# Part of the dense tokens of a PEER layer gather their expert rows, four slots of a token on the partitions

## The chip, the cores and the metric

The kernel runs on 1 core of one Trainium2 chip. The metric is the device time of one execution in microseconds. Runs of the kernel before took 3018.54 us at the median of three (3012.81 to 3020.27). The profile shows one execution; durations, waits and clocks below come from it.

Names: TensorE is PE, its weight loads PEld, VectorE is DVE, ScalarE is ACT, GpSimd is POOL, SyncE is SP. DMAs issued by SP and by POOL share 16 DMA engines.

## The reference, cut to what matters

The reference is an encoder of two layers on 512 tokens of width 1024. A layer is an input projection, two groups of attention heads, an output projection, a layer norm, a PEER feed-forward and another layer norm. The change touches the PEER part:

```python
q = (xc @ wq).reshape(PEER_CHUNK, PEER_HEADS, 2, half)
sc = jnp.einsum('chpd,hpnd->chpn', q, sub_keys, ...)
s1, i1 = lax.top_k(sc[:, :, 0], PEER_TOPK)
s2, i2 = lax.top_k(sc[:, :, 1], PEER_TOPK)
...                                   # the best 16 of 16 x 16 sums: top_s, eidx
g = jax.nn.softmax(top_s, axis=-1)
u_sel = jnp.take(u, eidx, axis=0)
a = jax.nn.gelu(jnp.einsum('chkd,cd->chk', u_sel, xc, ...), approximate=False)
w = (g * a).astype(x.dtype)
v_sel = jnp.take(v, eidx, axis=0)
return jnp.einsum('chk,chkd->cd', w, v_sel)
```

There are 8 heads with 16 experts each, so 128 slots a token, out of 16384 experts. Each expert has one row of u and one of v, of 1024 floats.

## The kernel before, in words

The 512 tokens are four chunks of 128. Chunk 0 (`gat`) takes its PEER part by **gathering**; chunks 1 to 3 (`dense`, 384 tokens, `ND`) take it **dense**, over all 16384 experts in 128 blocks (`NB`) of 128.

Dense, for a block: TensorE multiplies the block's u rows with the tokens and ScalarE takes the gelu, which gives a tile `ge` of 128 experts by 384 tokens (`acts`, L841 to L859). The gates of the chosen experts stand in a table G in DRAM, block by block, zero where an expert was not chosen; `w_` = G times `ge` (L1085). `w_` is the stationary operand that combines the block's v rows into six PSUM banks `accb`, 128 tokens by 512 columns each, over all 128 blocks (`combine`, L1043 to L1050). To keep fp32 precision with the fast fp32r matmul, u, v, `w_` and the tokens are split in a high and a low part, and three products are summed: a block has 8 x 3 matmuls of 384 columns for the activations and 6 x 3 of 512 columns for the combination. ScalarE casts the high parts (uh L850, vh L1081, wh L1088) and VectorE subtracts for the low ones (ul L851, vl L1082, wl L1089).

G is written by `spread` (L893): 48 steps of 8 tokens, one-hot products by VectorE, 16 matmuls of 128 f16 columns, copies by ScalarE into a tile `stg`, and a DMA of each group of 32 tokens. During the spread the activations of the first 24 blocks (`LEAD`) run ahead, and a ring of 24 `ge` buffers holds them. In the main loop (L1057) the activations of block b+24 come beside the combination of block b, so blocks 0 to 103 have 42 matmuls and blocks 104 to 127 only 18. The last six are held back to the end.

Gathering, for chunk 0: 256 indirect DMAs in a layer (L1005), issued by POOL. Each brings one row of u or v per token, token t on partition t, 128 rows of 4 KB. For u a VectorE instruction multiplies and sums the row with the token (`ujob`, L1009), for v another adds the weighted row to one of two accumulators (`vjob`, L1017). Before them comes the ranking of chunk 0 (`rank`, L966, 37 steps on VectorE). Four buffers (`slots`, L956) are used in turn.

The order: ranking steps, 128 u jobs, 128 v jobs and 7 closing steps form one list of 300 `jobs` (L1032 to L1034). `pace` (L1055) says how many of them follow each block: weight 4 for blocks 1 to 103, 1 for 104 to 121. All jobs of a block stand behind its `wl`. VectorE's order in the main loop is the written one (`manual_schedule`, L1056); the other engines' queues are ordered by the framework's planner. The u and v blocks come by SP, two blocks to a DMA of 1 MB (L844, L884), with four buffers `wst` for both; G by one DMA for four blocks (L888).

Of the kernel before, what the change touches and what calls it, by code (L numbers as in the profile page):

```python
# [48 lines left out]
def encoder_kernel(ctx: ExitStack, tc: tile.TileContext, x, ln_in_g, ln_in_b, w_in, qn_g, kn_g, sink,  # L49
# [152 lines left out]
    for l in range(L):  # L202
# [638 lines left out]
        def acts():  # L841

            for g2 in range(NB // 2):
                ut = load_w(peer_ut[l, g2], "ut")  # L844
                for bi in range(2):
                    us = ut[:, bi * D:(bi + 1) * D]
                    b = mm_bank("ps_a")
                    uh = up.tile([P, KD, P], F32R, tag="uh", name="uh")
                    ul = up.tile([P, KD, P], F32R, tag="ul", name="ul")
                    act.copy(uh.rearrange(ff), us)  # L850
                    v.tensor_tensor(out=ul.rearrange(ff), in0=us, in1=uh.rearrange(ff).bitcast(F32), op=SUB)  # L851
                    for k in range(KD):
                        pe.matmul(b[:, :ND], uh[:, k, :], xTh[:, k, :], start=k == 0, stop=False)  # L853
# [39 lines left out]
        def spread():  # L893
            for c in dense:
                for tg in range(P // TG):
                    stg = (sp, lp)[tg % 2].tile([P, NB, TG], F32, tag="stg", name="stg", bufs=1)
                    for t8 in range(TG // 8):
# [12 lines left out]
                        v.tensor_tensor(out=o12, in0=bc(iota2[:, None, :, :], sh2), in1=bc(iu[:, :, None, :], sh2), op=EQ)  # L910
                        v.tensor_tensor(out=a_h, in0=o1, in1=tv(gh), op=MUL)
                        v.tensor_tensor(out=a_l[:, :3], in0=o1[:, :3], op=MUL,
                                        in1=bc(gl[:, o:o + 6].rearrange("p (q t) -> p q t", t=2)[:, :, None, :], [P, 3, P, 2]))
                        for t in range(2):
                            act.activation(a_l[:, 3, :, t], o1[:, 3, :, t], AF.Copy, scale=glf[:, o + 6 + t:o + 7 + t])
                        for q in range(2):
                            b = acc_bank("ps_g")
                            for t in range(4):
                                bs = b[:, t * P:(t + 1) * P]
                                r, e = q * 2 + t // 2, t % 2  # L920
                                pe.matmul(bs, o2[:, r, :, e], a_h[:, r, :, e], start=True, stop=False)  # L921
                                pe.matmul(bs, o2[:, r, :, e], a_l[:, r, :, e], start=False, stop=True)  # L922
# [36 lines left out]
        def slot():  # L959
            used[0] += 1  # L960
            return slots[:, used[0] % 4, :]
        for c in gat:
# [37 lines left out]
            acc = [ep.tile([P, D], F32, tag=f"gacc{i}", name="gacc", bufs=1) for i in range(2)]  # L1000
            ep.tile([P, 112], BF16, tag="line", name="line", bufs=1)

            def gather(src, j, idx=idx):
                t = slot()
                pool.indirect_dma_start(out=t, out_offset=None, in_=src,  # L1005
                                        in_offset=bass.IndirectOffsetOnAxis(ap=idx[:, j:j + 1], axis=0))
                return t

            def ujob(j, c=c, a_=a_, w_=w_, gather=gather):  # L1009
                t = gather(peer_u, j)  # L1010
                v.tensor_tensor_reduce(out=t, in0=t, in1=h[:, c, :], op0=MUL, op1=ADD, scale=1.0,  # L1011
                                       scalar=0.0, accum_out=a_[:, j:j + 1])
# [4 lines left out]
            def vjob(j, acc=acc, w_=w_, c=c, gather=gather):  # L1017
                t = gather(peer_v, j)
                if j < 2:
                    v.tensor_scalar(acc[j], t, w_[:, j:j + 1], None, op0=MUL)  # L1020
                else:
                    v.scalar_tensor_tensor(acc[j % 2], t, w_[:, j:j + 1], acc[j % 2], op0=MUL, op1=ADD)  # L1022
# [32 lines left out]
        pace = [0 if b < 1 or b >= NB - 6 else 4 if b < NB - LEAD else 1 for b in range(NB)]  # L1055
        with tc.manual_schedule(engines={mybir.EngineType.DVE}):  # L1056
            for g2 in range(NB // 2):  # L1057
                if g2 > 0:
# [7 lines left out]
                for bi in range(2):  # L1066
# [21 lines left out]
                    act.copy(wh, wf)  # L1088
                    v.tensor_tensor(out=wl, in0=wf, in1=wh.bitcast(F32), op=SUB)  # L1089
# [7 lines left out]
                    while done < want:  # L1097
                        f, j = jobs[done]
                        f(j)
                        done += 1  # L1100
# [82 lines left out]
```

## Time and profile before

| | value |
|---|---|
| median of three runs | 3018.54 us |
| the profiled execution | 3019.66 us, span 3017.9 us |
| PE busy, PEld busy | 98%, 90% |
| DVE, ACT, POOL busy | 81%, 43%, 27% |
| moved by DMA | 749.46 MB, 248 GB/s over the span |
| granted TensorE clock | 0.996 |

A row of instructions gives the line, the engine, the operation, the tile that is written and those that are read, and the shape; in a group, the count, the busy time, the mean time of one in ns, then the idle time of the engine just ahead of it and what ended that. Ends of matmuls are modelled, and consecutive ones overlap, so the time from one start to the next is what one costs. A window row gives the busy time of each engine in a stretch, the granted clock, the mean busy share of the 16 DMA engines and the GB/s.

### The profile page before, as it was taken

How to read it: one execution, taken by the hardware profiler on the slowest of the kernel's cores; microseconds unless marked ns; L12 is line 12 of the kernel's file. 1: busy time of each engine (PE TensorE's matmuls, PEld its weight loads, DVE VectorE, ACT ScalarE, POOL GpSimd, SP SyncE). 2: the span in 40 equal slices, each digit the busy share in tenths (PEclk: the TensorE clock that was granted, in tenths of full speed). 3: DMA queues.
4: the chain of work that ended last, by engine and by line, in shares of the span. 5: the costliest groups of instructions: out<-in, count | busy, mean ns of one | idle time of the engine just before them, and what ended most of it. 6: DMA issues, size and time to landing. Idle time of an engine off the chain costs nothing.

```text
span 3017.9 us, 47799 instructions
## 1 busy us (share of the span) xinstructions
PE 2952.6 (98%) x18034; PEld 2716.3 (90%) x18034; DVE 2435.1 (81%) x5084; ACT 1310.7 (43%) x2642; POOL 820.7 (27%) x524
## 2 busy tenths in 40 slices
PE   7999999999999999999999999999999999999998
PEld 7899899999999999998898998999999999998986
DVE  6777999778887888888777789997787887787887
ACT  4665168443333333333247641783433333333332
POOL 0000000015555555553000000000255555555630
PEclk9999999999999999999999999999999999999999
DMA  5014667659999989998420247775689989888982
GB/s 196 29 57 151 235 254 280 214 207 335 327 326 330 329 322 328 331 338 301 149 98 15 73 164 273 259 262 205 236 318 339 334 317 335 323 318 310 330 298 91
DMA packets 262232, 749.46 MB, mean 248 GB/s; under 512 B 19952, under 2 KB 130288, under 8 KB 231792
## 3 DMA queue, kind: packets, MB, share of 16 engines
q1 hardware_dynamic: 188272, 477.94, 44.4%
q0 software_dynamic: 73728, 268.47, 24.9%
q8 instruction: 141, 2.31, 0.3%
q14 instruction: 91, 0.75, 0.1%
HBM read 691.81 MB, written 54.53 MB: 247 GB/s over the span
## 4 chain that ended last, share of the span: by engine, by line
PE 85%; DVE 12%; ACT 1%; issue 1%; DMA 1%; SPq 0%; DVEq 0%; ACTq 0%
PE ps_a L855 12%; PE ps_a L854 12%; PE ps_a L853 12%; PE ff L1050 11%; PE ff L1048 11%; PE ff L1049 11%; PE ps_o L417 2%; PE ps_g L922 2%; PE ps_g L921 2%; DVE ix L573 1%; PE ps_pt L403 1%; PE ps_s L379 1%; DVE sv L571 1%; PE ps_m L447 1%; DVE wql L511 1%
## 5 line engine op out<-in xcount | busy, mean ns | idle before, releaser
L1005 POOL DMA_INDIRECT gt<-in_dram,idx x512 | 811.2, 1584 | 1913.5 <-ACT vh L1081 1206.4
L855 PE MATMUL ps_a<-xT,ul 128*128 128x384 f32 x2048 | 689.1, 336 | 1.8 <-DVE ul L851 1.8
L854 PE MATMUL ps_a<-xT,uh 128*128 128x384 f32 x2048 | 688.7, 336 | 0.0
L853 PE MATMUL ps_a<-xT,uh 128*128 128x384 f32 x2048 | 688.7, 336 | 0.0
L1048 PE MATMUL ff<-vh,wh 128*128 128x512 f32 x1440 | 561.3, 390 | 1.9 <-ACT wh L1088 1.9
L1050 PE MATMUL ff<-vh,wl 128*128 128x512 f32 x1440 | 562.6, 391 | 0.0
L1049 PE MATMUL ff<-vl,wh 128*128 128x512 f32 x1440 | 560.6, 389 | 0.0
L1081 ACT CAST vh<-vt 128x1024 fp32r<-128x1024 f32 x240 | 251.9, 1051 | 492.8 <-PE ff L1050 252.5
L854 PEld LDWEIGHTS ps_a<-xT,uh 128*128 128x128 f32 x2048 | 385.0, 188 | 9.6
L853 PEld LDWEIGHTS ps_a<-xT,uh 128*128 128x128 f32 x2048 | 385.2, 188 | 8.0
L855 PEld LDWEIGHTS ps_a<-xT,ul 128*128 128x128 f32 x2048 | 385.1, 188 | 2.1 <-DVE ul L851 2.1
L1082 DVE TENSOR_TENSOR vl<-vt,vh 128x1024 fp32r<-128x1024 f32 x240 | 293.5, 1223 | 108.7 <-ACT vh L1081 107.3
L1088 ACT CAST wh<-w 128x384 fp32r<-128x384 f32 x240 | 123.6, 515 | 575.8 <-DVE w L1085 575.8
L1022 DVE SCALAR_TENSOR_TENSOR gacc<-gt,gw,gacc 128x1024 f32<-128x1024 f32 x252 | 314.6, 1281 | 54.8 <-DMA gt<-in_dram,idx 54.3
L1011 DVE CUSTOM_DVE_ANT_0 gt<-gt,h 128x1024 f32<-128x1024 f32 x256 | 304.6, 1222 | 43.7 <-DMA gt<-in_dram,idx 43.4
L851 DVE TENSOR_TENSOR ul<-ut,uh 128x1024 fp32r<-128x1024 f32 x256 | 312.4, 1220 | 26.4 <-ACT uh L850 26.4
L1050 PEld LDWEIGHTS ff<-vh,wl 128*128 128x128 f32 x1440 | 270.5, 188 | 56.9
L850 ACT CAST uh<-ut 128x1024 fp32r<-128x1024 f32 x256 | 269.5, 1053 | 120.0 <-PE ps_a L854 112.4
L1048 PEld LDWEIGHTS ff<-vh,wh 128*128 128x128 f32 x1440 | 270.4, 188 | 50.9 <-ACT wh L1088 2.7
L1049 PEld LDWEIGHTS ff<-vl,wh 128*128 128x128 f32 x1440 | 270.5, 188 | 48.4
L1089 DVE TENSOR_TENSOR wl<-w,wh 128x384 fp32r<-128x384 f32 x240 | 134.0, 559 | 154.7 <-ACT wh L1088 154.7
L1085 DVE SCALAR_TENSOR_TENSOR w<-gg,ge 128x384 f32<-128x384 f32 x256 | 141.8, 554 | 0.0
(278 smaller groups left out, 4632.7 us busy)
## 6 DMA issues: line engine op xcount, KB each, us to landing
ut<-in_dram SPq DMA_DIRECT2D x128, 1024.0 KB
vt<-in_dram SPq DMA_DIRECT2D x128, 1024.0 KB
w_pq<-in_dram SPq DMA_DIRECT2D x48, 1024.0 KB
gg<-G SPq DMA_DIRECT2D x62, 768.0 KB
G<-stg SPq DMA_DIRECT2D x24, 1920.0 KB
w_o<-in_dram SPq DMA_DIRECT2D x24, 1024.0 KB
w_q<-in_dram SPq DMA_DIRECT2D x8, 1024.0 KB
gt<-in_dram,idx POOLq DMA_INDIRECT x512
```

The source lines that it names most:

```text
L850: act.copy(uh.rearrange(ff), us)
L851: v.tensor_tensor(out=ul.rearrange(ff), in0=us, in1=uh.rearrange(ff).bitcast(F32), op=SUB)
L853: pe.matmul(b[:, :ND], uh[:, k, :], xTh[:, k, :], start=k == 0, stop=False)
L854: pe.matmul(b[:, :ND], uh[:, k, :], xTl[:, k, :], start=False, stop=False)
L855: pe.matmul(b[:, :ND], ul[:, k, :], xTh[:, k, :], start=False, stop=k == KD - 1)
L1005: pool.indirect_dma_start(out=t, out_offset=None, in_=src, in_offset=bass.IndirectOffsetOnAxis(ap=idx[:, j:j + 1], axis=0))
L1011: v.tensor_tensor_reduce(out=t, in0=t, in1=h[:, c, :], op0=MUL, op1=ADD, scale=1.0, scalar=0.0, accum_out=a_[:, j:j + 1])
L1022: v.scalar_tensor_tensor(acc[j % 2], t, w_[:, j:j + 1], acc[j % 2], op0=MUL, op1=ADD)
L1048: pe.matmul(b, wh[:, cs], vh[:, ns], start=blk == 0, stop=False)
L1049: pe.matmul(b, wh[:, cs], vl[:, ns], start=False, stop=False)
L1050: pe.matmul(b, wl[:, cs], vh[:, ns], start=False, stop=blk == NB - 1)
L1082: v.tensor_tensor(out=vl, in0=vt[:, bi, :], in1=vh.bitcast(F32), op=SUB)
```

## The change

The last 32 tokens of chunk 3 (`NX` = 32) leave the dense activations and gather their rows, as chunk 0 does. Four slots of a token are brought at once: 32 tokens x 4 slots (`NQ` = 4) fill the 128 partitions, with slots 32q to 32q+31 of a token on partition group q. So 32 u gathers and 32 v gathers a layer serve them (`qujob`, `qvjob`). Before the loop the tokens, their indices and gates are copied to the four groups by 12 small DMAs. Each partition sums its own 32 slots in `qacc`; two fp32 matmuls (`qsum`) with a selection matrix `sel`, built once at the start, add the four groups and put the sum into the accumulator banks of chunk 3.

The activations have 352 columns (`NA`) in place of 384. The last 32 columns of `ge` are set to zero by POOL in each block, and the last group of G is set to zero in place of being spread: 44 steps in place of 48. `w_`, `wh`, `wl`, the reading of G and the combination keep all 384 tokens.

The list has 365 jobs: 32 qujobs; 37 ranking steps with 16 qvjobs between them; 16 qvjobs and two qsums; 128 u jobs, 128 v jobs, 6 closing steps. While chunk 0 is ranked, three buffers belong to the ranking, and the qvjobs use two (the last two of the ranking's 16 top steps end before a shared one is taken). After the ranking a fifth gather buffer is taken from the space of the former second accumulator; chunk 0's v jobs have one accumulator. Up to one job of a block is placed behind `ul` (`between`), another between `wh` and `wl`, and the rest behind the block's combination. The weights of `pace` are 3 for blocks 3 to 103 and 1 for 104 to 121.

```diff
+    NA = ND - NX
+    NQ = P // NX
...
+    sel = cp.tile([P, P], F32, name="sel")
+    v.tensor_scalar(sel, ident, 0.0, None, op0=MUL)
+    for q in range(NQ):
+        v.tensor_tensor(out=sel[:, P - NX:], in0=sel[:, P - NX:], in1=ident[:, q * NX:(q + 1) * NX], op=ADD)
...
+                    if between:
+                        between[0](len(gel) - LEAD)
                     for k in range(KD):
-                        pe.matmul(b[:, :ND], uh[:, k, :], xTh[:, k, :], start=k == 0, stop=False)
...
+                        pe.matmul(b[:, :NA], uh[:, k, :], xTh[:, k, :NA], start=k == 0, stop=False)
...
+                    pool.memset(ge[:, NA:], 0.0)
+                    act.activation(ge[:, :NA], b[:, :NA], AF.Gelu)
...
-        STEPS = ND // 8
+        STEPS = NA // 8
...
+                    if gi == NTG - 1:
+                        pool.memset(stg[:, :, TG - NX:], 0.0)
+                    for t8 in range((TG if gi < NTG - 1 else TG - NX) // 8):
...
+        to_rows(qc, *idx)
+        for q in range(NQ):
+            rs, js = slice(q * NX, (q + 1) * NX), slice(q * JQ, (q + 1) * JQ)
+            nc.sync.dma_start(qi[rs, :], idx[0][qr, js])
+            nc.sync.dma_start(hq[rs, :], h[qr, qc, :])
+            nc.sync.dma_start(qg[rs, :], gte[qr, qc, js])
+
+        def qujob(j):
+            t = gather(peer_u, qi[:, j:j + 1])
+            v.tensor_tensor_reduce(out=t, in0=t, in1=hq, op0=MUL, op1=ADD, scale=1.0,
+                                   scalar=0.0, accum_out=qa[:, j:j + 1])
+            if j == JQ - 1:
+                act.activation(qw, qa, AF.Gelu)
+                v.tensor_tensor(out=qw, in0=qw, in1=qg, op=MUL)
+
+        def qvjob(j, s):
+            t = gather(peer_v, qi[:, j:j + 1], s)
+            if j == 0:
+                v.tensor_scalar(qacc, t, qw[:, j:j + 1], None, op0=MUL)
+            else:
+                v.scalar_tensor_tensor(qacc, t, qw[:, j:j + 1], qacc, op0=MUL, op1=ADD)
+
+        def qsum(n):
+            ns = slice(n * 512, (n + 1) * 512)
+            pe.matmul(accb[qc, n], sel, qacc[:, ns], start=False, stop=False)
...
+                places_.append(lambda: ep.tile([P, D], F32, tag="gacc1", name="gt4", bufs=1))
...
-                if j < 2:
-                    v.tensor_scalar(acc[j], t, w_[:, j:j + 1], None, op0=MUL)
+                if j == 0:
+                    acc.append(ep.tile([P, D], F32, tag="gacc0", name="gacc", bufs=1))
+                    v.tensor_scalar(acc[0], t, w_[:, j:j + 1], None, op0=MUL)
                 else:
-                    v.scalar_tensor_tensor(acc[j % 2], t, w_[:, j:j + 1], acc[j % 2], op0=MUL, op1=ADD)
+                    v.scalar_tensor_tensor(acc[0], t, w_[:, j:j + 1], acc[0], op0=MUL, op1=ADD)
...
-            jobs += [(lambda j, ranks=ranks: next(ranks, None), j) for j in range(37)]
+            jobs += [(qujob, j) for j in range(JQ)]
+            rk = [(lambda j, ranks=ranks: next(ranks, None), j) for j in range(37)]
+            qv = [(lambda j: qvjob(j, 2 + j % 2 if j < 16 else None), j) for j in range(JQ)]
+            for i in range(37):
+                jobs += rk[i:i + 1] + (qv[i - 1:i] if 1 <= i < 17 else [])
+            jobs += qv[16:] + [(qsum, n) for n in range(2)]
...
+        def one(blk):
+            more(min(done[0] + 1, len(jobs) * sum(pace[:blk + 1]) // sum(pace)))
+
+        between.append(one)
+        pace = [0 if b < 3 or b >= NB - 6 else 3 if b < NB - LEAD else 1 for b in range(NB)]
...
                     act.copy(wh, wf)
+                    one(blk)
                     v.tensor_tensor(out=wl, in0=wf, in1=wh.bitcast(F32), op=SUB)
...
-                    want = len(jobs) * sum(pace[:blk + 1]) // sum(pace)
...
+                    more(len(jobs) * sum(pace[:blk + 1]) // sum(pace))
```

More of the change, by code (lines that the diff above doesn't have):

```diff
@@ L36 @@
 TG = 32
+NX = 32
 GB = 4
@@ L839, in encoder_kernel @@
         gel = []
+        between = []
         def acts():
@@ L851, in acts @@
                     v.tensor_tensor(out=ul.rearrange(ff), in0=us, in1=uh.rearrange(ff).bitcast(F32), op=SUB)
+                    if between:
+                        between[0](len(gel) - LEAD)
                     for k in range(KD):
-                        pe.matmul(b[:, :ND], uh[:, k, :], xTh[:, k, :], start=k == 0, stop=False)
-                        pe.matmul(b[:, :ND], uh[:, k, :], xTl[:, k, :], start=False, stop=False)
-                        pe.matmul(b[:, :ND], ul[:, k, :], xTh[:, k, :], start=False, stop=k == KD - 1)
+                        pe.matmul(b[:, :NA], uh[:, k, :], xTh[:, k, :NA], start=k == 0, stop=False)
+                        pe.matmul(b[:, :NA], uh[:, k, :], xTl[:, k, :NA], start=False, stop=False)
+                        pe.matmul(b[:, :NA], ul[:, k, :], xTh[:, k, :NA], start=False, stop=k == KD - 1)
                     ge = gp.tile([P, ND], F32, tag="ge", name="ge", bufs=LEAD)
-                    act.activation(ge, b[:, :ND], AF.Gelu)
+                    pool.memset(ge[:, NA:], 0.0)
+                    act.activation(ge[:, :NA], b[:, :NA], AF.Gelu)
                     gel.append(ge)
@@ L896, in spread @@
                     stg = (sp, lp)[tg % 2].tile([P, NB, TG], F32, tag="stg", name="stg", bufs=1)
-                    for t8 in range(TG // 8):
+                    gi = (c * P + tg * TG - T0) // TG
+                    if gi == NTG - 1:
+                        pool.memset(stg[:, :, TG - NX:], 0.0)
+                    for t8 in range((TG if gi < NTG - 1 else TG - NX) // 8):
                         gh, glf, gl, iT = flat[c]
@@ L957, in encoder_kernel, with slot, gather @@
         used = [0]
-        def slot():
+        places_ = [slots[:, i, :] for i in range(4)]
+        def slot(s=None):
+            if s is not None:
+                return slots[:, s, :]
             used[0] += 1
-            return slots[:, used[0] % 4, :]
-        for c in gat:
+            i = used[0] % len(places_)
+            if callable(places_[i]):
+                places_[i] = places_[i]()
+            return places_[i]
+        def gather(src, ix, s=None):
+            t = slot(s)
+            pool.indirect_dma_start(out=t, out_offset=None, in_=src,
+                                    in_offset=bass.IndirectOffsetOnAxis(ap=ix, axis=0))
+            return t
@@ L963, in encoder_kernel, with places, to_rows @@
+        def places(c):
             idx = ep.tile([P, J], I32, tag="idx", name="idx", bufs=1)
             fx = ep.tile([P, J], F32, tag="fx", name="fx", bufs=1)
+            return idx, fx
+        def to_rows(c, idx, fx):
+            v.tensor_scalar(fx, i1f[:, c, :], 128.0, float(l * NE), op0=MUL, op1=ADD)
+            v.tensor_tensor(out=idx, in0=fx, in1=i2f[:, c, :], op=ADD)
+        qc = dense[-1]
+        qr = slice(P - NX, P)
+        JQ = J // NQ
+        idx = places(qc)
+        ep.tile([P, J], F32, tag="ga", name="ga", bufs=1)
@@ new lines, in encoder_kernel @@
+        ep.tile([P, J], F32, tag="gw", name="gw", bufs=1)
+        qacc = ep.tile([P, D], F32, tag="gacc0", name="qacc", bufs=1)
+        hq = ep.tile([P, D], F32, tag="gacc1", name="hq", bufs=1)
+        ep.tile([P, 112], BF16, tag="line", name="line", bufs=1)
+        qi = ep.tile([P, JQ], I32, tag="qi", name="qi", bufs=1)
+        qg, qa, qw = (ep.tile([P, JQ], F32, tag=t, name=t, bufs=1) for t in ("qg", "qa", "qw"))
+        to_rows(qc, *idx)
[4 more added lines that the diff above has]
+            nc.sync.dma_start(qg[rs, :], gte[qr, qc, js])
@@ L966, in rank @@
+        def qsum(n):
+            ns = slice(n * 512, (n + 1) * 512)
+            pe.matmul(accb[qc, n], sel, qacc[:, ns], start=False, stop=False)
+        for c in gat:
+            idx, fx = places(c)
             def rank(c=c, idx=idx, fx=fx):
-                sx = slot()
+                sx = ep.tile([P, D], F32, tag="gacc1", name="sx", bufs=1)
                 n = 2 * PH * TK
@@ L978, in rank @@
                     yield from top_keys(st, hd, sc[hd // 4][:, hd % 4])
-                big = [slot() for _ in range(3)]
+                big = [slot(i) for i in range(3)]
                 tl = dict(ge=big[0].bitcast(F16), t1=big[1].bitcast(F16))
@@ L994, in rank @@
                 yield from soft(c, c + 1)
-                v.tensor_scalar(fx, i1f[:, c, :], 128.0, float(l * NE), op0=MUL, op1=ADD)
-                v.tensor_tensor(out=idx, in0=fx, in1=i2f[:, c, :], op=ADD)
+                to_rows(c, idx, fx)
+                places_.append(lambda: ep.tile([P, D], F32, tag="gacc1", name="gt4", bufs=1))
             ranks = rank()
@@ L999, in encoder_kernel, with ujob @@
             w_ = ep.tile([P, J], F32, tag="gw", name="gw", bufs=1)
[L1000 to L1010, printed above, removed]
+            acc = []
+            def ujob(j, c=c, a_=a_, w_=w_, idx=idx):
+                t = gather(peer_u, idx[:, j:j + 1])
                 v.tensor_tensor_reduce(out=t, in0=t, in1=h[:, c, :], op0=MUL, op1=ADD, scale=1.0,
@@ L1015, in ujob, with vjob @@
                     v.tensor_tensor(out=w_, in0=w_, in1=gte[:, c, :], op=MUL)
-            def vjob(j, acc=acc, w_=w_, c=c, gather=gather):
-                t = gather(peer_v, j)
-                if j < 2:
-                    v.tensor_scalar(acc[j], t, w_[:, j:j + 1], None, op0=MUL)
+            def vjob(j, acc=acc, w_=w_, c=c, idx=idx):
+                t = gather(peer_v, idx[:, j:j + 1])
+                if j == 0:
+                    acc.append(ep.tile([P, D], F32, tag="gacc0", name="gacc", bufs=1))
+                    v.tensor_scalar(acc[0], t, w_[:, j:j + 1], None, op0=MUL)
                 else:
-                    v.scalar_tensor_tensor(acc[j % 2], t, w_[:, j:j + 1], acc[j % 2], op0=MUL, op1=ADD)
+                    v.scalar_tensor_tensor(acc[0], t, w_[:, j:j + 1], acc[0], op0=MUL, op1=ADD)
             def tail(c=c, acc=acc):
-                v.tensor_tensor(out=acc[0], in0=acc[0], in1=acc[1], op=ADD)
-                yield
                 hc = h[:, c, :]
@@ L1031, in encoder_kernel @@
             steps = tail()
-            jobs += [(lambda j, ranks=ranks: next(ranks, None), j) for j in range(37)]
+            jobs += [(qujob, j) for j in range(JQ)]
[4 more added lines that the diff above has]
+            jobs += qv[16:] + [(qsum, n) for n in range(2)]
             jobs += [(ujob, j) for j in range(J)] + [(vjob, j) for j in range(J)]
-            jobs += [(lambda j, steps=steps: next(steps, None), j) for j in range(7)]
+            jobs += [(lambda j, steps=steps: next(steps, None), j) for j in range(6)]
         g_2 = bload(ln2_g[l], D, "ln_g")
@@ L1053, in encoder_kernel, with more @@
         parts = []
-        done = 0
-        pace = [0 if b < 1 or b >= NB - 6 else 4 if b < NB - LEAD else 1 for b in range(NB)]
+        done = [0]
+        def more(want):
+            while done[0] < want:
+                f, j = jobs[done[0]]
+                done[0] += 1
+                f(j)
+        def one(blk):
+            more(min(done[0] + 1, len(jobs) * sum(pace[:blk + 1]) // sum(pace)))
+        between.append(one)
+        pace = [0 if b < 3 or b >= NB - 6 else 3 if b < NB - LEAD else 1 for b in range(NB)]
         with tc.manual_schedule(engines={mybir.EngineType.DVE}):
@@ L1095, in encoder_kernel @@
                         parts.append((blk, wh, wl, vh, vl))
-                    want = len(jobs) * sum(pace[:blk + 1]) // sum(pace)
[L1097 to L1100, printed above, removed]
+                    more(len(jobs) * sum(pace[:blk + 1]) // sum(pace))
         for c in dense:
```

3 lines of the change are left out of this document (1 added, 2 removed).

## The prediction

> **What bounds the kernel now.** I read the busy shares first, then the chain that ended last, then the stages of layer 0 in a table of windows, and last the rows of single instructions. The page:
>
> ```profile
> PE 2952.6 (98%) x18034; PEld 2716.3 (90%) x18034; DVE 2435.1 (81%) x5084; ACT 1310.7 (43%) x2642; POOL 820.7 (27%) x524
> ...
> PEclk9999999999999999999999999999999999999999
> ...
> PE 85%; DVE 12%; ACT 1%; issue 1%; DMA 1%; SPq 0%; DVEq 0%; ACTq 0%
> ```
>
> TensorE is 98% busy at full granted clock and 85% of the chain. A busy PE is not yet a bound PE, so the stages (columns: stretch, length, busy time and count of PE, PEld, DVE, ACT, POOL, then clock, DMA share and GB/s):
>
> ```profile
> 403.00:555.00 152.00, 152.00 (x1355) 142.01 (x1354) 138.37 (x175) 119.01 (x247) 0.00 (x0) 1.00 0.72 268
> 555.00:660.00 105.00, 105.00 (x534) 95.75 (x533) 82.27 (x280) 41.94 (x55) 0.00 (x0) 1.00 0.49 170
> 660.00:1412.00 752.00, 752.00 (x3826) 686.89 (x3826) 606.12 (x748) 275.30 (x369) 394.11 (x255) 1.00 0.92 328
> 1412.00:1486.00 74.00, 74.00 (x327) 60.94 (x326) 59.50 (x86) 28.27 (x39) 4.34 (x3) 1.00 0.62 205
> ```
>
> They are the spread (the 48 steps that write G, with 24 expert blocks of matmul ahead), blocks 0 to 13 with the ranking of chunk 0, the 90 blocks with gathers, and the last blocks without activations. PE has no gap in any of them. But the third, half the time, runs DMA at 0.92 and DVE at 0.81 (606 of 752): neither is far behind. Starts of consecutive matmuls give their true price:
>
> ```profile
> 800.48 0.33 PE L853 MATMUL ps_a<-xT,uh 128*128 128x384 f32 x1
> ...
> 802.04 0.33 PE L853 MATMUL ps_a<-xT,uh 128*128 128x384 f32 x1
> ...
> 803.08 0.39 PE L1048 MATMUL ff<-vh,wh 128*128 128x512 f32 x1
> ...
> 804.90 0.39 PE L1050 MATMUL ff<-vh,wl 128*128 128x512 f32 x1
> ...
> 287.26 0.28 PE L551 MATMUL ps_pq<-xT,wql 128*128 128x256 f32 x1
> 287.38 0.28 PE L549 MATMUL ps_pq<-xT,wqh 128*128 128x256 f32 x1
> ...
> 449.38 0.22 PE L921 MATMUL ps_g<-ah,o 128*128 128x128 f16 x1
> ...
> 449.96 0.22 PE L922 MATMUL ps_g<-al,o 128*128 128x128 f16 x1
> ```
>
> The first pair lies nine starts apart, the second eight, the third one, the last ten: 384 columns go every 0.173 us, 512 every 0.227, 256 every 0.12, the 128 of f16 every 0.058. For the wide ones that is 13 ns and 0.417 ns a column. A block of 24 activation and 18 combining matmuls is 24 x 0.173 + 18 x 0.227 = 8.24 us. The weight load does not hold it: at 256 columns the pairs already go at 0.12.
>
> **The change, part by part.** *Narrower activations.* 352 columns: 0.160 us, so 0.32 us less per block, 7.92. Over 128 blocks and 2 layers that is 82 us, if PE stays the bound everywhere.
>
> *Spread.* 44 steps in place of 48. A step is 16 matmuls of 0.058 us, so four are 3.7 us of PE; 24 blocks ahead save 7.7. DVE, 138 of 152 us busy there, loses three instructions a step:
>
> ```profile
> L910 DVE TENSOR_TENSOR o<-iota,fl 128x2048 f16<-128x2048 f16 x48 | 56.6, 1220 | 0.6 <-PE ps_g L922 0.3
> L911 DVE TENSOR_TENSOR ah<-o,fl 128x1024 f16<-128x1024 f16 x48 | 32.9, 686 | 0.0
> ...
> L912 DVE TENSOR_TENSOR al<-o,fl 128x768 f16<-128x768 f16 x48 | 26.5, 553 | 0.0
> ```
>
> That is 2.46 us a step, 9.8 in all, so DVE does not hold the gain of 11.4 back by more than 1.6. I take 10 us a layer.
>
> *More gathers, sooner.* 64 more per layer, 320 in place of 256. Jobs go from 300 to 365. The old pace weights sum to 430, so a block at weight 4 takes 2.79 jobs; the new sum to 321, so one at weight 3 takes 3.41. Jobs 0 to 31 gather u for the 32 tokens (blocks 3 to 11), then come 37 ranking steps with 16 v gathers between them (12 to 27), then almost nothing but gathers to block 103 (76 blocks). Their bytes:
>
> ```profile
> q1 hardware_dynamic: 188272, 477.94, 44.4%
> q0 software_dynamic: 73728, 268.47, 24.9%
> ...
> ut<-in_dram SPq DMA_DIRECT2D x128, 1024.0 KB
> vt<-in_dram SPq DMA_DIRECT2D x128, 1024.0 KB
> ...
> gg<-G SPq DMA_DIRECT2D x62, 768.0 KB
> ...
> gt<-in_dram,idx POOLq DMA_INDIRECT x512
> ```
>
> A gather is 268.47 / 512 = 0.524 MB. ut and vt serve two blocks each and gg four: 1.245 MB a block. Before: 1.245 + 2.79 x 0.524 = 2.71 MB in 8.24 us, 329 GB/s, which is the 328 of the row. After: 1.245 + 3.41 x 0.524 = 3.03 MB; 7.92 us would need 383 GB/s. What can the queues do? Full busy is 477.94 MB in 44.4% of 3017.9 us, 357 GB/s, on average. Stretches that are already full, of 20 and of 8.25 us:
>
> ```profile
> 700.00:720.00 20.00, 20.00 (x106) 18.58 (x105) 14.70 (x21) 7.56 (x10) 11.08 (x7) 1.00 0.98 354
> 740.00:760.00 20.00, 20.00 (x104) 18.37 (x103) 15.99 (x22) 7.08 (x9) 9.77 (x8) 1.00 1.00 375
> 1100.00:1120.00 20.00, 20.00 (x102) 18.03 (x101) 16.02 (x17) 7.45 (x10) 9.13 (x7) 1.00 1.00 354
> ...
> 1000.00:1008.25 8.25, 8.25 (x44) 7.54 (x43) 6.96 (x11) 3.01 (x4) 5.37 (x4) 1.00 0.99 379
> 1008.25:1016.50 8.25, 8.25 (x44) 7.54 (x43) 5.45 (x10) 3.00 (x4) 3.21 (x4) 1.00 1.04 373
> 1066.00:1074.25 8.25, 8.25 (x44) 7.54 (x43) 5.79 (x7) 3.01 (x4) 2.68 (x2) 1.00 1.02 395
> ```
>
> The long ones mean 361, the short ones 382. I take the middle, 372: the backlog will be steady, but a stretch picked for being full flatters. So a gather block lasts 3.03 / 0.372 = 8.15 us, set by DMA and no longer by PE: 0.09 less than before, not 0.32. The ends are 8.51 (357 GB/s) and 7.92 (PE).
>
> *DVE.* One more job per 1.6 blocks, and jobs moved between ul and vl and between w and wl:
>
> ```profile
> L1011 DVE CUSTOM_DVE_ANT_0 gt<-gt,h 128x1024 f32<-128x1024 f32 x128 | 152.4, 1222 | 21.1 <-DMA gt<-in_dram,idx 20.9
> L1022 DVE SCALAR_TENSOR_TENSOR gacc<-gt,gw,gacc 128x1024 f32<-128x1024 f32 x121 | 151.0, 1282 | 17.2 <-DMA gt<-in_dram,idx 16.9
> ...
> L1082 DVE TENSOR_TENSOR vl<-vt,vh 128x1024 fp32r<-128x1024 f32 x92 | 112.6, 1224 | 46.9 <-ACT vh L1081 46.7
> ...
> L1089 DVE TENSOR_TENSOR wl<-w,wh 128x384 fp32r<-128x384 f32 x91 | 50.8, 559 | 58.3 <-ACT wh L1088 58.3
> ```
>
> These are groups of 660 to 1412. DVE is busy 606 / 752 x 8.24 = 6.64 us a block. It waits 0.64 for wh, 0.51 for vh and 0.42 for gathers. 0.62 more jobs of about 1.2 us make 7.39. A job in each gap covers the first two waits, which are worth nothing while PE is the bound and are needed now. Gather waits at today's rate are 0.52, in all 7.91: DVE just fits under 8.15. Behind a late gather stand, on DVE in its written order, vl, w and wl of the block, and behind these PE. The single accumulator in place of two makes adjacent v jobs dependent; 1.28 against a spacing of about 1.2 is under 0.1 us a block, within the 0.24 left.
>
> *Five buffers, and POOL.* The fifth keeps the time a buffer may take round at 5 / 3.41 blocks of 8.15, 12.0 us, where 4 / 2.79 x 8.24 was 11.8. That time is needed:
>
> ```profile
> 1002.77 1.68 POOL L1005 DMA_INDIRECT gt<-in_dram,idx  x1 [2.27 <-DVE ga L1011]
> ...
> 1010.89 1.25 DVE L1011 CUSTOM_DVE_ANT_0 gt<-gt,h 128x1024 f32<-128x1024 f32 x1 [0.28 <-DMA gt<-in_dram,idx]
> ...
> 1434.15 1.05 POOL L221 TENSOR_TENSOR tabs<-sin,gk 128x256 f32<-128x256 f32 x1
> ```
>
> Issue to use is 8 us with the queues full. POOL issues 3.41 x 1.55 (394.11 / 255) = 5.3 us a block, below 8.15. The new memset of 32 columns costs at most the 1.05 of the nearest POOL row; it waits for the buffer that w frees, and the next gather stands behind it on POOL. From nothing, where it runs when the buffer is already free, to an added gather wait on every block; I take nothing, the price stands with the third rival. The memset of a whole stg, 16 times that row's elements, is 1 to 17 us under the activation blocks that end the spread.
>
> *The small rest.* qsum: an fp32 matmul of 256 columns is two instructions of 0.216 us:
>
> ```profile
> 244.33 3.46 PE ps_m L447 x16
> ```
>
> So 512 columns are 0.87, two per layer 1.7 us; PE stands behind the last v job of the 32 tokens, once, covered by DVE's lead of about a block. SP issues 12 small DMAs before the loop, which wait for the indices; loads of vt and ut stand behind: 0 to 4 us at about 0.35 each, with the stg memset I take 1. The DVE work for the selection matrix is about 1 us once. In blocks 104 to 121 20 jobs remain in place of 12: 10 us more DVE on 59.5 of 74; I take 2.
>
> *Sum per layer:* spread -10; blocks 0 to 2, PE-bound, -1; blocks 3 to 11 at 8.15, -0.8; blocks 12 to 27 -2.5 (below); 76 gather blocks -6.8; rest +4.7. That is -16.4, two layers -32 with the 1 us. For blocks 12 to 27 the row is
>
> ```profile
> 640.00:660.00 20.00, 20.00 (x102) 18.18 (x102) 18.08 (x31) 8.01 (x11) 0.00 (x0) 1.00 0.44 156
> ```
>
> where the last ranking steps run: DVE 18.08 / 20 x 8.24 = 7.45 us a block, less 3.29 without jobs, over 2.79 steps is 1.5 us each. At 3.41 a block, with no v gathers between them, DVE needs 8.4 for about six blocks (+0.13 each); the other ten go at 7.92. The profiled execution took 3019.66 us, 1.1 above the median: 2987 or 2988 so, 2986 beside the median.
>
> **Rivals.** *1, PE keeps the pace.* The short full windows (382 on average, 395 once) say that 383 GB/s can be had; against it, these follow on idle stretches. Then 85 blocks gain 0.32: -27 in place of -7.6 a layer, 2948. The Trainium skill, "Perfetto Trace Analysis", section Roofline, says a lone core may draw more than its 358 GB/s share, to about 120%; by it DMA would not bind and this rival would hold; the trace agrees only in short windows.
>
> *2, slower: DMA stays at its average.* In the same 85 blocks at 357 GB/s, 8.51 us: +0.27 each, +23 a layer; with -8.8 for the rest +14, in all 3048. It decides from 368 GB/s down, where a block costs the old 8.24. For it: the average of both queues over the run (the gathers' 24.9% gives 357 too). The Trainium skill, "DMA: Bandwidth & Descriptors", Specifications, gives about 358 GB/s as a core's HBM limit; by that a block would be 8.47. The trace's 375 over 20 us stands above it.
>
> *3, gathers land later still.* If DVE waits 2.5 times today's 0.52 a block, it needs 8.69: +34 over 76 blocks, +24 a layer, 3067. It decides from 1.6 times. For it: 8 us of latency already. Against: jobs no longer three in a row.
>
> *4, a draw.* Gather waits, or DMA at 366 to 370, put blocks at 8.2 to 8.33: little but the spread and the early blocks gains, 2995 to 3017.
>
> *5, narrower matmuls save nothing* (a load of weights lasts 0.188 us): the 0.12 spacing at 256 columns speaks against it; 3030 or more.
>
> **How the numbers follow.** Forecast (blocks of 8.0 to 8.2; 2960 to 2995) 0.40; rival 1 0.12; rival 4 0.18; rival 2 (blocks from 8.33 to 8.6) 0.18; rival 3 0.09; rival 5 0.03. A measurement here can tell about 0.3%, 9 us, from no change. Forecast, rival 1 and a third of rival 4 (under 3009) give faster 0.58; the rest of rival 4 and the low edge of rival 2 (to 3027) same 0.20; the others slower 0.22. The range takes rivals 1 and 2 in: 2945 to 3052.
>
> **What would show it.** Matmuls of 352 columns 0.160 us apart; windows of the gather stretch at a DMA share near 1.0 and 365 to 380 GB/s; PE with gaps there that end on DVE, and DVE's waits on gt grown while those for wh and vh are gone; blocks of 8.1 to 8.2 us. Wrong if PE shows no gaps there (rival 1), if the share is 1.0 below 365 GB/s (rival 2), or if DMA is below 0.95 while DVE waits on gt (rival 3).

## The result and the profile after

The changed kernel takes 2964.6 us at the median of four runs (2963.46 to 2969.65), the kernel before on the same chip 3015.68. The ratio is 0.9833, 95% interval 0.9813 to 0.9853: 1.7% faster, 51 us. The forecast was 2986. Its sign and its range held; the likeliest case did not come, as the stages show. One of the six later runs of the changed kernel (e10_again below) took 10129 us at a granted clock of 0.278 and is left out of its median and ratio.

The page of the changed kernel: busy shares, DMA rate by slices of 74 us, the queues, and the chain that ended last.

```profile
PE 2881.2 (97%) x17914; PEld 2635.4 (89%) x17914; DVE 2543.5 (86%) x5261; ACT 1284.6 (43%) x2612; POOL 928.6 (31%) x910
...
GB/s 199 30 58 138 234 263 273 323 316 239 317 364 374 381 387 379 378 392 376 173 100 16 74 141 268 256 269 331 312 234 323 375 378 385 383 378 384 380 368 93
...
q1 hardware_dynamic: 189424, 479.06, 44.8%
q0 software_dynamic: 92160, 335.59, 29.6%
...
PE 73%; DVE 14%; DMA 8%; issue 2%; ACT 2%; POOL 1%; SPq 0%; DVEq 0%; ACTq 0%; POOLq 0%
...
PE ff L1120 10%; PE ff L1118 10%; PE ff L1119 10%; PE ps_a L865 9%; PE ps_a L863 9%; PE ps_a L864 9%; DMA gt<-in_dram,qi 6%; PE ps_o L424 2%; PE ps_g L936 1%; PE ps_g L935 1%; DVE ix L580 1%; PE ps_pt L410 1%; PE ps_s L386 1%; DVE sv L578 1%; DMA G<-stg 1%
```

The slices in the middle of a layer carry 374 to 392 GB/s. DMA is now on the chain with 8%, and 6 of these are `gt<-in_dram,qi`, the gathers of the 32 tokens. Chunk 0's gathers, 512 of the 640, are not listed there. Three stages of layer 0, in the columns of the windows before:

```profile
403.00:543.50 140.50, 140.41 (x1293) 132.26 (x1293) 126.39 (x160) 111.13 (x230) 3.89 (x4) 1.00 0.71 264
543.50:672.60 129.10, 119.71 (x599) 105.04 (x598) 95.57 (x162) 40.07 (x58) 55.18 (x53) 0.97 0.89 322
...
800.00:1372.00 572.00, 572.00 (x3021) 519.13 (x3021) 521.52 (x659) 209.62 (x286) 340.75 (x314) 1.00 1.00 379
```

In the long gather stretch PE has no gap (572.00 of 572.00), at a DMA share of 1.00. In the second stage, the first 15 blocks, it stands still for 9.4 us of 129.1. So the gain came where DMA was forecast to take most of it, and a loss came where little change was forecast.

The start of `w` on DVE marks the blocks, and a forecast per stage can be set beside them. The first fence is the kernel before, the second the changed one: blocks 0, 3, 12, 28, 103 and 127 of layer 0.

```profile
550.55 0.55 DVE L1085 SCALAR_TENSOR_TENSOR w<-gg,ge 128x384 f32<-128x384 f32 x1
...
570.25 0.56 DVE L1085 SCALAR_TENSOR_TENSOR w<-gg,ge 128x384 f32<-128x384 f32 x1
...
644.58 0.55 DVE L1085 SCALAR_TENSOR_TENSOR w<-gg,ge 128x384 f32<-128x384 f32 x1
...
777.20 0.55 DVE L1085 SCALAR_TENSOR_TENSOR w<-gg,ge 128x384 f32<-128x384 f32 x1
...
1395.64 0.55 DVE L1085 SCALAR_TENSOR_TENSOR w<-gg,ge 128x384 f32<-128x384 f32 x1
...
1485.90 0.55 DVE L1085 SCALAR_TENSOR_TENSOR w<-gg,ge 128x384 f32<-128x384 f32 x1
```

```profile
543.52 0.56 DVE L1166 SCALAR_TENSOR_TENSOR w<-gg,ge 128x384 f32<-128x384 f32 x1 [3.65 <-DMA gg<-G]
...
566.60 0.55 DVE L1166 SCALAR_TENSOR_TENSOR w<-gg,ge 128x384 f32<-128x384 f32 x1
...
645.39 0.55 DVE L1166 SCALAR_TENSOR_TENSOR w<-gg,ge 128x384 f32<-128x384 f32 x1
...
774.50 0.55 DVE L1166 SCALAR_TENSOR_TENSOR w<-gg,ge 128x384 f32<-128x384 f32 x1
...
1371.59 0.55 DVE L1166 SCALAR_TENSOR_TENSOR w<-gg,ge 128x384 f32<-128x384 f32 x1
...
1460.41 0.55 DVE L1166 SCALAR_TENSOR_TENSOR w<-gg,ge 128x384 f32<-128x384 f32 x1
```

| layer 0 | forecast, us | measured, us | us a block, before and after |
|---|---|---|---|
| up to block 0 (spread) | -10 | -7.0 | |
| blocks 0 to 2 | -1 | +3.4 | 6.57, 7.69 |
| blocks 3 to 11 | -0.8 | +4.5 | 8.26, 8.75 |
| blocks 12 to 27 | -2.5 | -3.5 | 8.29, 8.07 |
| blocks 28 to 102 | -6.8 | -21.3 | 8.25, 7.96 |
| the rest (measured: blocks 103 to 127) | +4.7 | -1.4 | |
| sum | -16.4 | -25.5 | |

Of the 4.7 that were reckoned for the rest, 2 belong to the blocks behind 103; the two sums (1.7) and SP's queue with the memset (1) fall into rows above.

### The profile page after: what moved, and what is told of

The parts are those of the page before. It is cut to its first block, busy times and chain, and to the rows that moved or that the text cites. A ratio compares the mean times of both kernels' runs of the same rounds, so it can differ in the third digit from the quotient of the medians.

```text
span 2962.8 us, 48878 instructions
## 1 busy us (share of the span) xinstructions
PE 2881.2 (97%) x17914; PEld 2635.4 (89%) x17914; DVE 2543.5 (86%) x5261; ACT 1284.6 (43%) x2612; POOL 928.6 (31%) x910
## 3 DMA queue, kind: packets, MB, share of 16 engines
q1 hardware_dynamic: 189424, 479.06, 44.8%
q0 software_dynamic: 92160, 335.59, 29.6%
## 4 chain that ended last, share of the span: by engine, by line
PE 73%; DVE 14%; DMA 8%; issue 2%; ACT 2%; POOL 1%; SPq 0%; DVEq 0%; ACTq 0%; POOLq 0%
PE ff L1120 10%; PE ff L1118 10%; PE ff L1119 10%; PE ps_a L865 9%; PE ps_a L863 9%; PE ps_a L864 9%; DMA gt<-in_dram,qi 6%; PE ps_o L424 2%; PE ps_g L936 1%; PE ps_g L935 1%; DVE ix L580 1%; PE ps_pt L410 1%; PE ps_s L386 1%; DVE sv L578 1%; DMA G<-stg 1%
## 5 line engine op out<-in xcount | busy, mean ns | idle before, releaser
L984 POOL DMA_INDIRECT gt<-in_dram,idx x512 | 695.8, 1359 | 416.3 <-DVE gacc L1089 193.2
L865 PE MATMUL ps_a<-xT,ul 128*128 128x352 f32 x2048 | 665.8, 325 | 6.4 <-DVE ul L859 6.4
L863 PE MATMUL ps_a<-xT,uh 128*128 128x352 f32 x2048 | 666.0, 325 | 5.0 <-ACT uh L858 5.0
L864 PE MATMUL ps_a<-xT,uh 128*128 128x352 f32 x2048 | 664.2, 324 | 0.0
L867 POOL MEMSET ge<- 128x32 f32 x256 | 31.3, 132 | 1145.1 <-PE ps_o L424 481.3
L1089 DVE SCALAR_TENSOR_TENSOR gacc<-gt,gw,gacc 128x1024 f32<-128x1024 f32 x254 | 326.1, 1284 | 20.7 <-DMA gt<-in_dram,idx 19.1
L1077 DVE CUSTOM_DVE_ANT_0 gt<-gt,h 128x1024 f32<-128x1024 f32 x256 | 310.6, 1220 | 16.8 <-DMA gt<-in_dram,idx 16.1
L984 POOL DMA_INDIRECT gt<-in_dram,qi x128 | 183.6, 1434 | 232.6 <-DVE qacc L1030 94.3
```

Source lines behind the costliest of these rows:

```text
L863: pe.matmul(b[:, :NA], uh[:, k, :], xTh[:, k, :NA], start=k == 0, stop=False)
L864: pe.matmul(b[:, :NA], uh[:, k, :], xTl[:, k, :NA], start=False, stop=False)
L865: pe.matmul(b[:, :NA], ul[:, k, :], xTh[:, k, :NA], start=False, stop=k == KD - 1)
L984: pool.indirect_dma_start(out=t, out_offset=None, in_=src, in_offset=bass.IndirectOffsetOnAxis(ap=ix, axis=0))
L1089: v.scalar_tensor_tensor(acc[0], t, w_[:, j:j + 1], acc[0], op0=MUL, op1=ADD)
```

## The experiments

All ratios are to the kernel before, timed on the same chip. In the row of the stretch from 850 to 1350 us, the matmul count over 42 is the number of blocks; the changed kernel's is

```profile
850.00:1350.00 500.00, 500.00 (x2645) 454.45 (x2644) 459.81 (x581) 184.78 (x253) 303.85 (x278) 1.00 1.00 381
```

63.0 blocks of 7.94 us. Two theories stood: PE sets this pace and DMA follows, or DMA gives just this.

**e1_wide: the matmuls at 384 columns again, gathers kept.**

```diff
-                        pe.matmul(b[:, :NA], uh[:, k, :], xTh[:, k, :NA], start=k == 0, stop=False)
+                        pe.matmul(b[:, :ND], uh[:, k, :], xTh[:, k, :ND], start=k == 0, stop=False)
...
```

> The changed kernel with the activation matmuls back at 384 columns (the 32 extra columns are computed and not read; gathers, spread, job order stay). If the narrower matmul is the whole gain and PE paces the gather blocks: blocks 28 to 103 go back from 7.96 to 8.24 us, and the 24 blocks ahead too, so about 0.31 us in 105 to 128 blocks of two layers, +65 to +80 us on 2964.6, at 3030 to 3045, slower than the kernel before, because the early blocks keep their loss. If the gain came from the new places of the jobs or from the shorter spread, the time stays under 3000.

Measured: 3027.0 us, ratio 1.0045 (1.0033 to 1.0058).

```profile
850.00:1350.00 500.00, 500.00 (x2547) 457.01 (x2547) 444.08 (x570) 180.98 (x245) 280.27 (x267) 1.00 0.98 367
```

60.6 blocks, 8.25 us, PE again without a gap. The narrower matmul is worth 62 us of the whole, just under the 65 to 80 expected and more than all of the gain; without it the gathers leave a loss of 0.45%.

**e2_n320: 320 columns, nothing gathered for the 32 tokens more that are left out.**

```diff
-                        pe.matmul(b[:, :NA], uh[:, k, :], xTh[:, k, :NA], start=k == 0, stop=False)
+                        pe.matmul(b[:, :NA - 32], uh[:, k, :], xTh[:, k, :NA - 32], start=k == 0, stop=False)
...
-                    act.activation(ge[:, :NA], b[:, :NA], AF.Gelu)
+                    act.activation(ge[:, :NA - 32], b[:, :NA - 32], AF.Gelu)
```

> The changed kernel with 320 columns in the activation matmuls and the gelu; 32 more columns of each activation tile are zero, so the PEER part of 32 more tokens is left out and nothing is gathered for them. DMA bytes, DVE work and job order stay. If PE is the bound of the gather blocks and DMA has room above 381 GB/s: blocks at 7.60 us (24 x 0.147 + 18 x 0.227), about 399 GB/s, and about -70 us, 2895. If DMA or DVE already set the 7.96: blocks stay at 7.85 to 7.96, only the blocks with few gathers gain, about -15 to -25 us, 2940 to 2950.

Measured: 2938.06 us, ratio 0.9755 (0.9731 to 0.9779), 27 us less than the changed kernel, where 15 to 25 or about 70 had been expected.

```profile
850.00:1350.00 500.00, 494.31 (x2695) 440.72 (x2694) 461.83 (x580) 175.21 (x255) 324.51 (x280) 1.00 1.01 385
```

PE now has gaps. Blocks take 7.8 us (500 x 42 / 2695), not 7.60, at a DMA share of 1.01 and 385 GB/s. DVE is no fuller than in the changed kernel. So PE did set the pace at 352 columns, with the next bound only about 0.15 us a block behind (7.94 against 7.79). The run shows DMA full there. Late gathers, which hold PE up through DVE's order, may have a share in that bound; the run does not separate the two.

**e3_end: all jobs behind `wl`, as before.**

```diff
-        between.append(one)
...
-                    one(blk)
```

> The changed kernel with all jobs of a block behind its wl, as before. If DVE fits only because jobs cover its waits: 7.39 us of work plus 0.64 for wh and 0.5 for gathers is 8.5 us a block, +0.5 us over 75 blocks of two layers, +75 us, 3040. If DVE's lead of about a block absorbs these waits: 7.39 plus 0.64 is near 8.05, +5 to +20 us, 2970 to 2985.

Measured: 3062.73 us, ratio 1.0168 (1.0144 to 1.0192): slower than the kernel before, and 98 us more than the changed kernel, where 75 had been the higher of the two forecasts.

```profile
850.00:1350.00 500.00, 485.06 (x2527) 434.02 (x2526) 442.28 (x564) 170.77 (x243) 322.05 (x265) 1.00 0.97 363
```

Blocks take 8.31 us. The groups of the same stretch, with idle time and releaser at the end:

```profile
L865 PE MATMUL ps_a<-xT,ul 128*128 128x352 f32 x480 | 157.6, 328 | 14.9 <-DVE ul L859 14.6
...
L1077 DVE CUSTOM_DVE_ANT_0 gt<-gt,h 128x1024 f32<-128x1024 f32 x119 | 141.0, 1221 | 15.5 <-DMA gt<-in_dram,idx 15.2
...
L1169 DVE TENSOR_TENSOR wl<-w,wh 128x384 fp32r<-128x384 f32 x60 | 33.8, 564 | 37.8 <-ACT wh L1168 37.2 <-issue 0.6
```

With `wl` first in line again, DVE stands before it for `wh`, 0.62 us a block (37.2 over 60), then for gathers, and PE in turn waits 14.6 us for DVE's `ul`. DVE with its waits has become the bound. PE, whose work did not change, now has gaps (485.06 of 500). By the starts of `w`, blocks 28 to 102 take 29 and 33 us more than in the changed kernel in the two layers; most of the rest lies in blocks 3 to 27 and behind block 103, where the jobs have moved as well.

**e4_four: four buffers throughout.**

```diff
-                places_.append(lambda: ep.tile([P, D], F32, tag="gacc1", name="gt4", bufs=1))
```

> The changed kernel with four gather buffers throughout. If the time that a buffer takes round is the limit: 7.5 us from issue to landing plus 1.2 on DVE and about 1 to 1.5 until the next issue is 10 us, four buffers give 3.41 gathers in 8.5 us, +0.55 us over 75 blocks of two layers, +80 us, 3045. If the queues and not the buffers set the time to landing, it shrinks with fewer in flight and the blocks stay within 0.1 us: +0 to +15 us, 2965 to 2980.

Measured: 3085.13 us, ratio 1.0234 (1.0207 to 1.0261).

```profile
850.00:1350.00 500.00, 468.73 (x2379) 408.02 (x2378) 409.82 (x532) 154.91 (x225) 280.56 (x249) 0.99 0.93 342
```

8.8 us a block with DMA at 0.93, so it is the buffers and not the queues. By the starts of `w`, blocks 28 to 102 take 61 and 58 us more than in the changed kernel in the two layers, nearly all of the 120 us between the two. In the list of waits of this stretch (total, times, longest) DVE waits for gathers, and PE behind it for wh and wl:

```profile
DVE gt L1076 <- DMA gt<-in_dram,idx: 58.5, 41, 4.2
DVE gacc L1088 <- DMA gt<-in_dram,idx: 31.0, 24, 4.5
PEld ff L1117 <- ACT wh L1168: 24.5, 18, 3.1
PEld ff L1119 <- DVE wl L1170: 21.3, 30, 1.7
```

**e9_place: everything but the 32 tokens** (384 columns, 48 steps, no new gathers; five buffers, new places and weights).

```diff
-    NA = ND - NX
+    NA = ND
...
-            jobs += [(qujob, j) for j in range(JQ)]
...
+            jobs += rk
```

> All of the change but the 32 tokens: 384 columns, 48 spread steps and no gathers for chunk 3, with five buffers, one accumulator, jobs between the parts of a block and the new weights. If PE paces the blocks at 8.24 us in the kernel before, new places and buffers are worth nothing there: ratio 0.997 to 1.003 to the kernel before. If the waits of DVE that they cover cost something there too: faster by 10 us or more.

Measured: 3012.39 us, ratio 1.0002 (0.9992 to 1.0011).

```profile
850.00:1350.00 500.00, 500.00 (x2548) 457.23 (x2547) 398.93 (x482) 182.97 (x245) 198.77 (x169) 1.00 0.91 329
```

The same places and buffers whose absence costs 98 to 120 us beside the gathers are worth nothing here, with 2.79 jobs a block and wide matmuls: where PE has no gap there is nothing to cover.

**e6_noq: no gathers, small DMAs and sums for the 32 tokens** (their PEER part is left out; the narrow matmuls stay).

```diff
-            jobs += [(qujob, j) for j in range(JQ)]
...
-            nc.sync.dma_start(qi[rs, :], idx[0][qr, js])
...
+            jobs += rk
```

> The changed kernel without the 64 gathers, the 12 small DMAs and the two sums per layer: the PEER part of the 32 tokens is left out. Jobs are 299 at the same weights, 2.79 a block. If the gathers cost only the early blocks (8.8 in place of 7.92 in blocks 3 to 11, 7.7 in place of 6.6 in 0 to 2): 12 us a layer and 2 for the sums, 28 us less, 2935 to 2940, with gather blocks at 7.92 to 7.96 still. If they also held the gather blocks, these fall by more than 0.04 us and the time is under 2930.

Measured: 2930.32 us, ratio 0.9723 (0.9710 to 0.9736).

```profile
850.00:1350.00 500.00, 500.00 (x2645) 454.50 (x2644) 415.29 (x492) 187.06 (x253) 215.59 (x239) 1.00 0.94 344
```

The stretch has the 2645 matmuls of the changed kernel. The 64 gathers a layer cost it nothing there, and nearly all of their 34 us lie elsewhere.

**Where the 34 us lie.** By the starts of `w` in layer 0, blocks 0 to 2 take 15.9 us in e6_noq and 23.1 in the changed kernel, and blocks 3 to 11 take 71.2 and 78.8. That is 15 us in this layer. SP's queue around the first blocks, before and after:

```profile
545.37 0.33 SPq L158 DMA_DIRECT2D ut<-in_dram  x1
...
555.03 1.29 SPq L158 DMA_DIRECT2D ut<-in_dram  x1
```

```profile
538.77 0.61 SPq L1013 DMA_DIRECT2D qi<-idx  x1
539.43 1.33 SPq L1014 DMA_DIRECT2D hq<-h  x1
...
550.32 0.59 SPq L1015 DMA_DIRECT2D qg<-gte  x1
551.01 0.53 SPq L161 DMA_DIRECT2D ut<-in_dram  x1
```

The row at 545.37 and the one at 551.01 are the same load, the 14th of ut in the layer, which brings blocks 26 and 27. It goes out 5.2 us ahead of the first `w` before and 7.5 behind it after. The 12 small DMAs, with one load of gg and one write of G among them, take SP's queue for 12 us, where 0.35 each had been reckoned, and this load stands behind them. DVE's `ul` for block 26 then waits 9.74 us for its cast, which stands on ACT behind a cast of vh that itself waits 3.6 us for PE; the shares of the two are not separated:

```profile
559.25 1.22 DVE L859 TENSOR_TENSOR ul<-ut,uh 128x1024 fp32r<-128x1024 f32 x1 [9.74 <-ACT uh L858]
```

Later, in blocks 3 to 11, the chain of the changed kernel (start, length) goes through single gathers:

```profile
583.10 9.97 DMA gt<-in_dram,qi
...
601.24 10.06 DMA gt<-in_dram,qi
```

There are four buffers there, the fifth coming only after the ranking.

**e5_pooldma: the small DMAs issued by POOL.**

```diff
-            nc.sync.dma_start(qi[rs, :], idx[0][qr, js])
+            nc.gpsimd.dma_start(qi[rs, :], idx[0][qr, js])
...
```

> The changed kernel with the 12 small DMAs (indices, tokens and gates of the 32) issued by POOL in place of SP. If they hold up SP's queue (12 us from 538.8 to 551.0, with the next load of ut behind them): that load goes out about 5 us sooner, blocks 0 to 3 fall from 7.7 to about 6.6 us, and the time falls by 5 to 8 us, 2957 to 2960. If the load is late because of the bytes of G in the queues and not because of SP: within 2 us of the changed kernel.

**e7_five_early: a fifth buffer for the 32 u gathers too**, in the space of `qacc`, which is used only after them.

```diff
-        qacc = ep.tile([P, D], F32, tag="gacc0", name="qacc", bufs=1)
+        places_.append(ep.tile([P, D], F32, tag="gacc0", name="gt4q", bufs=1))
+        qacc = []
...
             if j == JQ - 1:
+                places_.pop()
...
             if j == 0:
-                v.tensor_scalar(qacc, t, qw[:, j:j + 1], None, op0=MUL)
+                qacc.append(ep.tile([P, D], F32, tag="gacc0", name="qacc", bufs=1))
+                v.tensor_scalar(qacc[0], t, qw[:, j:j + 1], None, op0=MUL)
```

> The changed kernel with a fifth gather buffer for the 32 u gathers of blocks 3 to 11 too (the space of their accumulator, which is used only after them). If four buffers are too few at 3.41 gathers a block, as they were in the later blocks (8.76 us with four, 7.96 with five): blocks 3 to 11 fall from 8.8 to about 8.0 us, 7 us a layer, -14 us, 2951. If DMA, still busy with G, is the limit there: within 3 us of the changed kernel.

**e8_both** has both edits, **e10_again** is the changed kernel on the same chip as e8_both.

> The changed kernel with both: the 12 small DMAs issued by POOL, and the fifth gather buffer in blocks 3 to 11. If the two losses stand one after the other (SP's queue in blocks 0 to 2, buffers in 3 to 11), the gains add: 4 to 7 us and 16 us, about 2940, ratio 0.975 to 0.977 to the kernel before, blocks 0 to 2 at 6.1 and 3 to 11 at 8.0. If the late start only hid part of the second loss, or the sooner start meets fuller queues, it stays at 0.978.

> The changed kernel once more, as the measure for the small differences on the same chip: ratio 0.982 to 0.985 to the kernel before; blocks 3 to 11 at 8.7 to 8.9 us, 28 to 102 at 7.96.

| kernel | us | ratio, interval |
|---|---|---|
| e10_again | 2964.09 | 0.9835 (0.9822 to 0.9848) |
| e5_pooldma | 2957.74 | 0.9818 (0.9805 to 0.9832) |
| e7_five_early | 2945.54 | 0.9781 (0.9767 to 0.9794) |
| e8_both | 2940.26 | 0.9757 (0.9744 to 0.9769) |

In e5_pooldma the interval touches that of the changed kernel, so its time alone would not decide. Its rows do. SP's queue sends the 14th load of ut at 533.99, 17 us sooner, and on DVE the `w` of blocks 0 and 3 stand 18.10 us apart, where they stood 23.08 (543.52 to 566.60):

```profile
533.99 0.39 SPq L161 DMA_DIRECT2D ut<-in_dram  x1
```

```profile
544.63 0.56 DVE L1166 SCALAR_TENSOR_TENSOR w<-gg,ge 128x384 f32<-128x384 f32 x1 [5.99 <-DMA gg<-G]
...
562.73 0.55 DVE L1166 SCALAR_TENSOR_TENSOR w<-gg,ge 128x384 f32<-128x384 f32 x1
```

In e7_five_early blocks 3 to 11, by the same rows on DVE, take 71.94 us, 7.99 each, in place of 78.79:

```profile
567.02 0.55 DVE L1169 SCALAR_TENSOR_TENSOR w<-gg,ge 128x384 f32<-128x384 f32 x1
...
638.96 0.55 DVE L1169 SCALAR_TENSOR_TENSOR w<-gg,ge 128x384 f32<-128x384 f32 x1
```

Blocks 12 to 27 fall as well, by 4.7 us in layer 0 and 2.2 in layer 1; no run separates the reason.

The window from 560 to 640 us, of the changed kernel and then of e7_five_early:

```profile
560.00:640.00 80.00, 77.70 (x395) 68.55 (x396) 66.30 (x99) 25.32 (x38) 41.58 (x38) 0.98 0.96 349
```

```profile
560.00:640.00 80.00, 78.43 (x413) 70.57 (x412) 71.22 (x106) 26.84 (x39) 41.68 (x39) 1.00 1.02 387
```

With four buffers DMA carried 349 GB/s there, and with five 387, so its rate was not the limit: the buffers were.

The two gains add up within 2 us (6 and 19, together 24): e8_both, 2940.26 us, is 2.4% faster than the kernel before. They do not fall quite where they were expected: in layer 0 its blocks 0 to 2 take 6.64 us each (6.1 expected), its blocks 3 to 11 7.71 (8.0 expected). What is left of the gathers' cost, 10 us against e6_noq, was not followed further.

## Why the prediction was right, and where it was wrong

**Narrower activations: right.** Matmuls of 352 columns start 0.160 us apart (eight starts, changed kernel):

```profile
517.14 0.32 PE L863 MATMUL ps_a<-xT,uh 128*128 128x352 f32 x1
...
518.42 0.32 PE L865 MATMUL ps_a<-xT,ul 128*128 128x352 f32 x1
```

Rival 5 fell with it.

**More gathers: the step that failed.** "So a gather block lasts 8.15 us, set by DMA and no longer by PE" rested on 372 GB/s, the middle between long and short full stretches. DMA gave 381 at the pace of PE, 367 in e1_wide where PE asked for no more, and 385 in e2_n320 where the queues were full and PE had gaps. The term was mis-sized by about 3%; as demand lies at 383, that decided which resource paces 75 blocks. So rival 1 came true in the gather blocks, with the sign that had been named for it, no gaps of PE: 7.96, not 8.15, which is 14.5 us more in layer 0 than the likeliest case gave. The rule of the Trainium skill ("Perfetto Trace Analysis", Roofline) that a lone core may draw more than its 358 GB/s share holds here, by 6 to 8% in the rows above; its 120%, called the practical ceiling there, was not reached in any row shown. A slip beside it: 3.03 MB at 357 GB/s is 8.49 us, not 8.51, so rival 2 ends near 3044.

**DVE: right in size.** 459.81 us over 63.0 blocks is 7.30 a block, against 7.39; the groups show its waits:

```profile
L1077 DVE CUSTOM_DVE_ANT_0 gt<-gt,h 128x1024 f32<-128x1024 f32 x113 | 137.3, 1220 | 12.6 <-DMA gt<-in_dram,idx 12.5
L1089 DVE SCALAR_TENSOR_TENSOR gacc<-gt,gw,gacc 128x1024 f32<-128x1024 f32 x101 | 129.6, 1283 | 12.6 <-DMA gt<-in_dram,idx 11.7 <-DVE wl L1171 0.4
...
L1163 DVE TENSOR_TENSOR vl<-vt,vh 128x1024 fp32r<-128x1024 f32 x63 | 76.9, 1221 | 14.6 <-ACT vh L1162 14.2
...
L1171 DVE TENSOR_TENSOR wl<-w,wh 128x384 fp32r<-128x384 f32 x63 | 34.8, 552 | 0.0
```

Gathers 0.38 us a block (0.52 reckoned), vh 0.23 where its wait was to be covered, wh gone; in all 7.91, the sum that was reckoned, though from other terms. The signs said that waits on gt would grow; they did not. That the covered waits "are worth nothing while PE is the bound and are needed now" is what e9_place (nothing) and e3_end (98 us, about 31 a layer of it in blocks 28 to 102) show. In e3_end DVE is busy 7.35 a block and waits 0.62 for wh and 0.25 for u gathers: 8.22 of the 8.31. Rival 3 did not come.

**Five buffers: right for the late blocks, wrong for the early ones.** The round of 12 us for five was needed, as e4_four shows. But the working priced blocks 3 to 11 at the 8.15 of the blocks with five, and the kernel has four there: 4 / 3.41 blocks of 7.92 is 9.3 us, and single gathers took 10. That is the +4.5 in place of -0.8: e7_five_early, with five, takes 2.4 us less there than the kernel before.

**The small rest: SP's price was wrong.** "0 to 4 us at about 0.35 each" is 12 us of SP's queue for 12 DMAs, and about 5 us of it landed on blocks 0 to 2, as e5_pooldma shows (18.10 in place of 23.08). The spread gave 7.0 in place of 10: the first w now waits 3.65 us for gg, which follows the last write of G. The memset of a whole stg, reckoned at 1 to 17 us, measured 3.5 (groups of POOL, changed kernel) and lies under the activation blocks:

```profile
L910 POOL MEMSET stg<- 128x4096 f32 x2 | 7.0, 3517 | 0.4 <-POOL ge L867 0.4
```

So the total was 21 us too high. In layer 0 the gather blocks gave 14.5 us more than the likeliest case and the rest 6.1 more (-1.4 where +4.7 was reckoned), blocks 12 to 27 1.0 more; the spread and blocks 0 to 11 gave 12.7 less. That is 9 us. From the last `w` of layer 0 to the last of layer 1 the gain was 28.1, 12 more than a layer's 16.4. The range held because rival 1 was in it, not because its likeliest case was right; and that 2964.6 lies within the likeliest case's own 2960 to 2995 is luck: without the 12.7 us a layer that the spread and the early blocks gave too little it would have been near 2939.

## What to carry to other kernels

When work moves from one full resource to others, price all the others at the new pace and ask by how little the next one fails: here PE at 7.94 us a block, DVE with its waits at 7.91 and the next bound at 7.79 lay within 2%, and the same placing of jobs was worth nothing with the wide matmuls and few gathers and about 100 us after. For a ring of buffers, compare the time that it gives (buffers over uses) with the time from issue to use, stage by stage, since its size can change from one stage to the next. Many small DMAs on the queue that also brings the next weights cost their issue time, and the load behind them pays it, here 17 us late.

## What the runs showed of the hardware

The rate per busy DMA time was no constant. 335.59 MB of gathers in 29.6% of 2962.8 us is 383 GB/s, where the kernel before had 357; the other queue went from 357 to 361 (479.06 MB in 44.8%). An average share over a run with gaps was thus no ceiling. Fuller queues alone do not explain it: e9_place, with the gathers of the kernel before and DMA at 0.91 in its stretch, had 369 (268.47 MB in 24.2% of 3010.5 us). What sets the rate stays open. SP's small DMAs between SBUF tiles took 0.5 to 1.4 us of its queue each, against 0.3 to 0.4 for most of its loads of 1 MB.
